# Where operands start modulo 128 bytes: x's transposed parts shifted by 16 bytes, some high parts of the weights by 48

## The chip, the cores and the metric

One core of one Trainium2 chip. The metric is the device time of one execution in microseconds (us), the median of several runs.

## The reference, cut to what matters

A two-layer decoder trunk over 256 positions of width 1024, in float32: latent attention and a PEER expert block, then sparse attention and a second PEER block, each followed by a layer norm.

```
def peer_ffn(x, w_q, subkeys, u, v):              # per 128 positions
    q = (xc @ w_q).reshape(PEER_CHUNK, PEER_HEADS, 2, PEER_DK // 2)
    sc = jnp.einsum("thpd,hpnd->thpn", q, subkeys)  # then top-k: 128 experts a position
    ...
    a = jax.nn.gelu(jnp.einsum("thkd,td->thk", u_e, xc))
    return jnp.einsum("thk,thkd->td", (g * a), v_e)
```

There are 16384 experts. The kernel doesn't gather the rows of u: it multiplies x with the whole table, 128 blocks of 128 experts, and does nearly the same with v.

## The kernel before, in words

**Split products.** Each float32 factor is held as a high part (a float32r copy, made by ScalarE in `_shi`, L119) and a low part (the rest, made by VectorE in `_slo`, L130). A product is high·high + high·low + low·high, three TensorE matmuls on float32r. The weights come as one stream of tiles of 128 x 1024 (`plan`), loaded into `raw`, split into tiles `hi` and `lo` of a ring of four each, and taken by `nxt`.

**x.** The transposed activations lie in the tile `hT` (`new_hT`, L174): for each of eight blocks k of 128 channels, 256 columns of the high part and then 256 of the low part.

**The stages with most matmuls.** In each of the two PEER blocks:

- *Query projection and narrow steps.* `proj_T` (L198) makes 24 matmuls a tile: the weight block is stationary (loaded into the array), 256 columns of `hT` stream past it. This form is used for the queries, for the first steps of u, and for most projections of the sparse attention.
- *Wide steps of u* (`u_step`, from the point where the routing tiles are given up). The high part of the weights meets both parts of x in one matmul of 512 columns: seven of them, then eight matmuls of 256 columns with the low part of the weights, then the eighth of 512.
- *Steps of v* (`v_mm`). Now x-side tiles `W` (128 x 384) are stationary, and 512 columns of `hi` or `lo` stream: ten matmuls a step.

TensorE works in program order, so a matmul of a later stage never starts before those ahead of it.

**Where things start.** A partition's memory is filled pool by pool, in multiples of 32 bytes, so a tile's start follows from the sizes ahead of it. In the built program, modulo 128 bytes: `hT` starts at 96, all `hi`, `lo`, `W`, `cT`, `raw` at 32, `oT` at 32 in the first and 96 in the second attention. Columns are taken in blocks of 128 (512 bytes), so each slice of a tile has the tile's own start modulo 128. *Distance* below means: the start of the stationary block that is loaded for the next matmul, less the start of the operand that streams in the present one, modulo 128 bytes. Before, it is 64 in every product of `hT` with `hi` or `lo`, and 0 in those of `cT` with `hi` or `lo` and of `W` with `hi` or `lo`.

Of the kernel before, what the change touches and what calls it, by code (L numbers as in the profile page):

```python
# [12 lines left out]
F32 = mybir.dt.float32  # L13
F32R = mybir.dt.float32r
# [10 lines left out]
P = 128  # L25
S = 256
D = 1024
KC = D // P
# [6 lines left out]
FIRST, NEXT = 44, 10  # L35
GT = 64
ND = S - GT
RING, LEAD = 6, 7
AHEAD = 12
GB = 0.8  # L40
# [3 lines left out]
class Kern:  # L44
# [5 lines left out]
    def plan(self):  # L50
        I, L = self.I, []
        self.v0s, self.spare, self.pairs = [], None, {}
        if "mla" in self.parts:
            L += [I["a_w_in"][k] for k in range(KC)]
            L += [I["a_wk"][i] for i in range(2)]
            L += [I["a_wq"][i] for i in range(3)]
            L += [I["a_wv"][i] for i in range(2)]
            L += [I["a_wq"][i] for i in range(3, 6)]
            L += [I["a_wo"][i] for i in range(KC)]
        for l in (0, 1):  # L60
            if l == 1 and "nsa" in self.parts:
                L += [I["s_wv"][i] for i in range(4)]
                L += [I["s_wT"][i] for i in range(4)]
                L += [I["b_wg"]]
                L += [I["s_wT"][i] for i in range(4, 8)]
                L += [I["b_wq"][i] for i in range(4)]
                L += [I["b_wq"][i] for i in range(4, 8)]
                L += [I["b_wo"][i] for i in range(KC)] + [I["b_wo"][i] for i in range(KC // 2)]
            if f"peer{l}" in self.parts:
                L += [I["p_wq"][l, i] for i in range(16)]  # L70
                L += [I["p_u"][l, (P - FIRST + j) % P] for j in range(P)]
                self.v0s.append(len(L))
                o = (len(L) - self.v0s[0]) % 4
                self.pairs.update((len(L) + j, I["p_v"][l, j:j + 2].rearrange("j i d -> i j d")) for j in range(o % 2, P - 1, 2))
                L += [I["p_v"][l, j] for j in range(P)]
        self.stream = L
        self.v0 = self.vb = self.v0s[0]
        self.si = 0
        self.sd = 0
        self.sh = 0  # L80
        self.sl = 0
        self.raws, self.his, self.los = {}, {}, {}
        self.share = False
        self.alt = {}
        self.later, self.now = [], 0
# [25 lines left out]
    def _shi(self, upto):  # L111
        while self.sh <= min(upto, len(self.stream) - 1):
            i = self.sh
            self._sdma(i, True)
            if i in self.alt:
                self.his[i], self.los[i] = self.alt.pop(i)()
            else:
                self.his[i] = self.shl.tile([P, self.raws[i].shape[-1]], F32R, tag="hi", name="hi")
            self.nc.scalar.copy(self.his[i], self.raws[i])  # L119
            self.sh += 1  # L120

# [52 lines left out]
    def new_hT(self):  # L174

        self.spare = None
        self.hTT = self.pers.tile([P, KC, 2, S], F32R, tag="hT", name="hT")
        self.hT = [self.hTT[:, :, i, :] for i in range(2)]

    def prep_tail(self):  # L180
# [261 lines left out]
    def peer(self, l):  # L442
        tc, nc, I = self.tc, self.nc, self.I
        self.v0 = self.v0s.pop(0)
        with ExitStack() as es:
            pool = lambda st, name: st.enter_context(tc.tile_pool(name=name, bufs=1, reuse_waits="tile"))


            A = [(pool(es, "slots0").tile([P, FIRST, ND], F32, name="A0"), P - FIRST, FIRST)]

            def slot(j):
                for x, j0, n in A:
                    if j0 <= j < j0 + n:
                        return x[:, j - j0, :]
# [5 lines left out]
            gat = pool(es, "gather")  # L460
            gidx = gat.tile([P, 2, P // 2], U32, name="gidx")
            ggate = gat.tile([P, P // 2], F32, name="ggate")
            gw = gat.tile([P, P // 2], F32, name="gw")
            gel = [gat.tile([P, 4], F32, name=f"gel{m}") for m in range(16)]
            gacc = gat.tile([P, D], F32, name="gacc")
            grow, gtable = {}, I["p_v"].rearrange("l j i d -> (l j i) d")
# [145 lines left out]
            def g_gen(hot):  # L612

                b4 = [P, 2, P, 2]
                for t0 in range(0, ND, 4):
                    while len(gq) == 2:
# [76 lines left out]
            for n in range(4, 17):  # L693
                cur = []
                if n < 16:
                    hi, lo = self.nxt()
# [39 lines left out]
            def u_fin(x):  # L736
# [12 lines left out]
                if n:  # L749
                    nc.scalar.activation(ps[:, 0:n], ps[:, 0:n], AF.Gelu)  # L750
                    due.append((y[:, 0:n], ps[:, 0:n]))
                if n < ND:
                    nc.scalar.activation(y[:, n:ND], ps[:, n:ND], AF.Gelu)  # L753
                if j % 4 == 0:
                    gst.append(gat.tile([P, 4, GT], F32, tag="gst", name="gst", bufs=2))
                nc.scalar.activation(gst[-1][:, j % 4, :], ps[:, ND:S], AF.Gelu)  # L756
                if j % 4 == 3:
# [8 lines left out]
            def w_hi(j):  # L766
                if j < P:
                    WW[j] = late[0].tile([P, 3 * P], F32R, tag="w", name="W", bufs=10) if late else W[0][:, j % 5, :]
                    nc.scalar.copy(WW[j][:, 0:ND], slot(j))  # L769

# [13 lines left out]
            for j in range(P):  # L784
                x = u_step(j)
                u_fin(pu)
                pu = x
                g_flush(2)
                run_side(1.6 if len(A) == 1 else GB)
                if not side and len(A) == 1:  # L790
                    es_r.close()
                    hot = self.pr8.tile([P, 2, 3, 2, P, 2], F16, tag="r8", name="hot")
                    A.append((self.pr8.tile([P, NEXT, ND], F32, tag="r8", name="A2"), 0, NEXT))
                    n = P - FIRST - NEXT
                    A.append((pool(es_1, "slots1").tile([P, n, ND], F32, name="A1"), NEXT, n))
                    side.append(g_gen(hot))
                if done["g"] == ND and j >= P - 3 and not W:
                    w_start()
# [44 lines left out]
            for j in range(P):  # L843
# [9 lines left out]
                hi, lo = self.nxt(j < P - 2)  # L853
# [54 lines left out]
    def mla(self, hN, gb):  # L908
# [3 lines left out]
        with es:  # L912
            pool = lambda *a, **k: es.enter_context(tc.tile_pool(*a, reuse_waits="tile", **k))
            mp = pool(name="mla", bufs=1)
# [2 lines left out]
            keep = pool(name="mkeep", bufs=4)  # L917
            cN = mp.tile([P, 2, 768], F32, name="cN")
            kpN = mp.tile([P, 2, 32], F32, name="kpN")
            cT = [mp.tile([P, 6, S], F32R, tag=f"cT{i}", name=f"cT{i}") for i in range(2)]  # L920
            qT = mp.tile([96, NH, S], F32, name="qT")
            kT = mp.tile([96, NH, S], F32, name="kT")
            vN = mp.tile([P, 2, D], F32, name="vN")
            oT = [mp.tile([P, KC, S], F32R, tag=f"oT{i}", name=f"oT{i}") for i in range(2)]
            gq = mp.tile([P, 6], F32, name="gq")
            rN = mp.tile([P, 2, 64], F32, name="rN")
# [9 lines left out]
            for k in range(KC):  # L936
                hi, lo = self.nxt(k <= KC - 3)
# [66 lines left out]
            for b in range(2):  # L1004
                hi, lo = self.nxt(False)
# [14 lines left out]
            for b in range(2):  # L1020
                hi, lo = self.nxt()
# [21 lines left out]
            for k in range(2):  # L1043
                hi, lo = self.nxt()
# [14 lines left out]
            for st in range(NH + 3):  # L1059
                self.tick()  # L1060
                h = st
                if h < NH:
                    s = self.ps()
                    q, k = qT[:, h, :], kT[:, h, :]
# [6 lines left out]
                if 0 <= h < NH:  # L1071
                    p, m = pr.pop(h)
# [7 lines left out]
                if 0 <= h < NH and h % 2 == 1:  # L1080
                    pvp = self.ps()
                    pp = [pts.pop(h - 1), pts.pop(h)]
                    for w in range(2):
                        for e in range(2):
                            o = pvp[64 * e:64 * e + 64, 0:S]
# [6 lines left out]
                if h < NH:  # L1092
# [4 lines left out]
                    p = prob.tile([P, 384], F32, tag="p", name="p")  # L1097
# [4 lines left out]
                if 0 <= h < NH:  # L1102
                    p, m = pr[h]
# [560 lines left out]
```

## Time and profile before

| | us |
|---|---|
| median of 3 runs | 1760.79 |
| lowest, highest | 1753.84, 1761.01 |
| the profiled execution | 1749.82 |
| its span, first to last instruction | 1748.0 |

The profiled execution has its own time, and its span leaves out 1.8 us around it. The rows below are read from this execution.

### The profile page before, as it was taken

The page shows a single profiled execution, that of the slowest core. Times are in us where ns is not written, and L with a number is a line of the kernel's source. Part 1 is how long each engine was busy: PE and PEld are TensorE (multiplying, and loading weights), DVE is VectorE, ACT ScalarE, POOL GpSimd, SP SyncE. Part 2 cuts the span into 40 slices and gives each one's busy share as a digit, 9 for nine tenths or more (in the row PEclk, how much of TensorE's full clock was granted, in tenths as well). Part 3 has the DMA queues.
Part 4 walks back from the last instruction along what each step waited for, and adds up shares of the span by engine and source line. Part 5 has one row for each costly group of instructions (what it writes and reads, how often), then busy time and mean ns, then how long its engine had stood idle before and what let it go on. Part 6 is the DMA issues. An engine that isn't in the chain of part 4 may idle for free.

```text
span 1748.0 us, 30707 instructions
## 1 busy us (share of the span) xinstructions
PE 1703.1 (97%) x10610; PEld 1478.1 (85%) x10610; DVE 1553.4 (89%) x3675; ACT 1042.9 (60%) x2267; POOL 481.4 (28%) x441
## 2 busy tenths in 40 slices
PE   7999999999999999999997999999999999999997
PEld 6879999888888788888785789998888888888886
DVE  5778988989998899999778789988899998999998
ACT  6646555766666555556466755556666666555554
POOL 2110002000001777761341210001000005777740
PEclk9999999999999999999999999999999999999999
DMA  7535667555556899999572265657555557999993
GB/s 246 169 128 195 193 204 261 186 178 181 187 183 251 309 391 370 367 360 332 179 268 67 95 206 176 205 184 275 176 181 186 184 183 290 401 383 369 361 363 110
DMA packets 118619, 416.66 MB, mean 238 GB/s; under 512 B 16032, under 2 KB 18112, under 8 KB 117376
## 3 DMA queue, kind: packets, MB, share of 16 engines
q1 hardware_dynamic: 88976, 322.60, 54.2%
q0 software_dynamic: 29488, 92.10, 14.1%
q8 instruction: 84, 1.38, 0.3%
q14 instruction: 71, 0.58, 0.1%
HBM read 400.49 MB, written 13.63 MB: 237 GB/s over the span
## 4 chain that ended last, share of the span: by engine, by line
PE 72%; issue 16%; DVE 6%; DMA 2%; ACT 2%; POOL 1%; SPq 0%; POOLq 0%; ACTq 0%; DVEq 0%
PE acc L196 36%; PE mm L196 35%; PE mm L223 1%; DVE lo L130 1%; DMA raw<-p_wq 1%; POOL actD L758 1%; DVE keep L130 1%; DMA xT<-xT 0%; POOL row L472 0%; ACT hi L119 0%; POOL gel L476 0%; DMA gel<-actD,gidx 0%; DVE gacc L486 0%; DVE W L774 0%; DMA actD<-gst 0%
## 5 line engine op out<-in xcount | busy, mean ns | idle before, releaser
L119 ACT CAST hi<-raw 128x1024 fp32r<-128x1024 f32 (+1 forms) x463 | 484.6, 1049 | 244.6 <-PE acc L196 99.8
L196 PE MATMUL mm<-hT,hi 128*128 128x256 f32 (+1 forms) x3360 | 612.8, 328 | 0.0
L130 DVE TENSOR_TENSOR lo<-raw,hi 128x1024 fp32r<-128x1024 f32 (+1 forms) x459 | 558.3, 1220 | 32.6 <-ACT hi L119 30.9
L196 PEld LDWEIGHTS mm<-hT,hi 128*128 128x128 f32 x3360 | 483.2, 188 | 46.3 <-issue 1.2
L196 PE MATMUL acc<-hi,W 128*128 128x512 f32 x1452 | 408.8, 390 | 0.0
L196 PEld LDWEIGHTS acc<-hi,W 128*128 128x128 f32 x1452 | 273.2, 188 | 57.0
L196 PEld LDWEIGHTS mm<-hT,lo 128*128 128x128 f32 x2376 | 306.7, 188 | 15.9
L196 PE MATMUL mm<-hT,lo 128*128 128x256 f32 x2376 | 320.0, 277 | 0.0
L196 PE MATMUL acc<-lo,W 128*128 128x512 f32 x968 | 299.6, 391 | 1.8 <-DVE lo L130 1.8
L758 POOL DMA_DIRECT2D actD<-gst x64 | 34.8, 544 | 783.9 <-ACT gst L756 783.9
L472 POOL DMA_INDIRECT row<-p_v,gidx x128 | 191.7, 1498 | 117.8 <-DVE gacc L486 79.9
L196 PEld LDWEIGHTS acc<-lo,W 128*128 128x128 f32 x968 | 181.7, 188 | 41.4 <-DVE lo L130 4.1
L119 ACT CAST hi<-spare 128x1024 fp32r<-128x1024 f32 x122 | 128.1, 1050 | 113.9 <-PE acc L196 100.8
L476 POOL DMA_INDIRECT gel<-actD,gidx x128 | 165.7, 1294 | 50.0 <-issue 36.6
L486 DVE SCALAR_TENSOR_TENSOR gacc<-row,gw,gacc 128x1024 f32<-128x1024 f32 x126 | 161.4, 1281 | 1.1
L130 DVE TENSOR_TENSOR lo<-spare,hi 128x1024 fp32r<-128x1024 f32 x122 | 148.8, 1220 | 5.4 <-ACT hi L119 4.5
L750 ACT ACTIVATE mm<-mm 128x192 f32<-128x192 f32 (+23 forms) x170 | 41.1, 242 | 122.4 <-DVE mm L748 122.4
L774 DVE TENSOR_TENSOR W<-A,W 128x128 fp32r<-128x128 f32 (+1 forms) x512 | 107.6, 252 | 1.8 <-ACT W L769 1.8
L748 DVE TENSOR_TENSOR mm<-mm,half 128x256 f32<-128x256 f32 x174 | 74.5, 428 | 15.4 <-ACT half L747 15.0
L769 ACT CAST W<-A 128x192 fp32r<-128x192 f32 x256 | 88.0, 345 | 0.0
L647 DVE SCALAR_TENSOR_TENSOR A<-acc,A 128x176 f32<-128x176 f32 (+16 forms) x268 | 56.1, 274 | 28.6 <-PE acc L196 25.6
L753 ACT ACTIVATE A<-mm 128x192 f32<-128x192 f32 (+23 forms) x244 | 67.3, 276 | 7.8 <-DVE mm L748 2.8
(275 smaller groups left out, 1759.1 us busy)
## 6 DMA issues: line engine op xcount, KB each, us to landing
raw<-p_u SPq DMA_DIRECT2D x256, 512.0 KB, 4.0
spare<-p_v SPq DMA_DIRECT2D x64, 1024.0 KB, 8.8
raw<-p_v SPq DMA_DIRECT2D x63, 1024.0 KB, 8.7
raw<-p_wq SPq DMA_DIRECT2D x32, 512.0 KB, 4.1
actD<-gst POOLq DMA_DIRECT2D x64, 128.0 KB, 3.9
raw<-b_wo SPq DMA_DIRECT2D x12, 512.0 KB, 3.8
raw<-a_wo SPq DMA_DIRECT2D x8, 512.0 KB, 4.6
raw<-s_wT SPq DMA_DIRECT2D x8, 512.0 KB, 5.6
```

The lines of the kernel that those rows point to most:

```text
L119: self.nc.scalar.copy(self.his[i], self.raws[i])
L130: e.tensor_tensor(self.los[i], raw, self.his[i].bitcast(F32), op=OP.subtract)
L196: self.nc.tensor.matmul(out, a, b, start=start, stop=stop)
L472: nc.gpsimd.indirect_dma_start(out=t, out_offset=None, in_=gtable, in_offset=bass.IndirectOffsetOnAxis(ap=gidx[:, 0, c:c + 1], axis=0))
L476: nc.gpsimd.indirect_dma_start(out=gel[c // 4][:, c % 4:c % 4 + 1], out_offset=None, in_=gplaces, in_offset=bass.IndirectOffsetOnAxis(ap=g ...
L486: nc.vector.scalar_tensor_tensor(gacc, t, gw[:, c:c + 1], gacc, op0=OP.mult, op1=OP.add)
L647: nc.vector.scalar_tensor_tensor(y, pv[:, j0:j0 + m], 1.0 / GS, y, op0=OP.mult, op1=OP.mult)
L748: nc.vector.tensor_tensor(ps[:, 0:S], ps[:, 0:S], t, op=OP.add)
L753: nc.scalar.activation(y[:, n:ND], ps[:, n:ND], AF.Gelu)
L758: nc.gpsimd.dma_start(self.actD[:, jj - 3:jj + 1, :], gst.pop())
L769: nc.scalar.copy(WW[j][:, 0:ND], slot(j))
L774: nc.vector.tensor_tensor(WW[j][:, o:o + c.stop - c.start], slot(j)[:, c], WW[j][:, c].bitcast(F32), op=OP.subtract)
```

## The change

It adds bytes ahead of some operands and moves no instruction: each engine has the same instructions in the same order with the same waits.

- `hT` gets 32 bytes more, and its data start 16 bytes into the tile.
- Each `hi` tile gets 128 bytes more. Where the tile's number is in the set `near`, the data start 48 bytes into it. `near` holds the stream's tiles of the first projection, of the value projections and output projections (`a_wv`, `s_wv`, `b_wo`), and of the wide steps of u that are prepared after the switch to them.
- The tile `gw` is given up: the gated factor of the gathered rows is written over `ggate`.
- Two pads of 64 bytes in the first attention.

With the growth of the tiles ahead, the starts modulo 128 bytes become: `hT` 112; `hi` 64, or 112 in `near`; `lo`, `raw` and `W` 64; `cT` 0; `oT` 64 and 0. In the built program the distances are then:

| product (streams, columns; loaded next) | before | after | matmuls |
|---|---|---|---|
| `hT` 512; `hi` of `near` | 64 | 0 | 1128 |
| `hT` 512; other `hi`, `lo`, other | 64 | 80 | 262 |
| `hT` 256; `hi`, `lo` | 64 | 80 | about 4150 |
| `hT` 256 with `lo`; `hi` of `near` | 64 | 0 | 168 |
| `cT` 256; `hi`, `lo` | 0 | 64 | 187 |
| `hi`, `lo` 512; `W` | 0 | 0 | 2556 |
| `hi` 512 or 288; `hT` | 64 | 0 or 48 | 151 |
| `lo` 512 or 288; `hT` | 64 | 48 | 77 |
| `hi`, `lo` 512; `cT`, `oT` | 0 or 64 | 0, 16 or 64 | 168 |

A distance of 80 modulo 128 is 48 bytes in the other direction.

```
+NEAR = 12
...
         self.v0s, self.spare, self.pairs = [], None, {}
+        self.near = set()
         if "mla" in self.parts:
+            self.near.update(range(KC))
             L += [I["a_w_in"][k] for k in range(KC)]
...
+            self.near.update(range(len(L), len(L) + 2))
             L += [I["a_wv"][i] for i in range(2)]
...
+                self.near.update(range(len(L), len(L) + 4))
                 L += [I["s_wv"][i] for i in range(4)]
...
+                self.near.update(range(len(L), len(L) + KC + KC // 2))
                 L += [I["b_wo"][i] for i in range(KC)] + [I["b_wo"][i] for i in range(KC // 2)]
...
-                self.his[i] = self.shl.tile([P, self.raws[i].shape[-1]], F32R, tag="hi", name="hi")
+
+                n, o = self.raws[i].shape[-1], NEAR if i in self.near else 0
+                self.his[i] = self.shl.tile([P, n + 32], F32R, tag="hi", name="hi")[:, o:o + n]
...
-        self.hTT = self.pers.tile([P, KC, 2, S], F32R, tag="hT", name="hT")
+        t = self.pers.tile([P, 2 * KC * S + 8], F32R, tag="hT", name="hT")
+        self.hTT = t[:, 4:4 + 2 * KC * S].rearrange("p (k a t) -> p k a t", k=KC, a=2)
...
-            gw = gat.tile([P, P // 2], F32, name="gw")
+            gw = ggate
...
                     es_r.close()
+                    self.near.update(range(self.si, self.v0))
...
+            mp.tile([P, 16], F32, name="pad")
             cT = [mp.tile([P, 6, S], F32R, tag=f"cT{i}", name=f"cT{i}") for i in range(2)]
...
+            mp.tile([P, 16], F32, name="pad2")
             oT = [mp.tile([P, KC, S], F32R, tag=f"oT{i}", name=f"oT{i}") for i in range(2)]
```

## Rows read from the trace of the kernel before

**Rows 1.** The page: busy time by engine, and TensorE's granted clock in tenths.

```profile
PE 1703.1 (97%) x10610; PEld 1478.1 (85%) x10610; DVE 1553.4 (89%) x3675; ACT 1042.9 (60%) x2267; POOL 481.4 (28%) x441
...
PEclk9999999999999999999999999999999999999999
```

**Rows 2.** The page's chain that ended last; the chain's longest piece in narrow steps.

```profile
PE 72%; issue 16%; DVE 6%; DMA 2%; ACT 2%; POOL 1%; SPq 0%; POOLq 0%; ACTq 0%; DVEq 0%
...
171.92 87.77 PE mm L196 x772
```

**Rows 3.** Busy us by window: narrow steps, wide steps, v of each layer.

```profile
core 0: us, PE busy (x) PEld busy (x) DVE busy (x) ACT busy (x) POOL busy (x), PEclk, DMA share, GB/s
172.00:262.00 90.00, 90.00 (x794) 90.00 (x795) 84.63 (x347) 49.40 (x101) 3.79 (x7) 1.00 0.64 198
300.00:400.00 100.00, 100.00 (x682) 87.28 (x681) 88.44 (x230) 66.89 (x188) 4.32 (x8) 1.00 0.59 193
580.00:700.00 120.00, 120.00 (x530) 99.35 (x530) 118.56 (x203) 68.55 (x105) 90.34 (x67) 1.00 1.00 383
1460.00:1680.00 220.00, 220.00 (x972) 182.25 (x971) 213.16 (x364) 125.83 (x194) 160.07 (x117) 1.00 0.98 368
```

**Rows 4.** Timeline of PE in a wide step: start us, us, what, how many.

```profile
401.68 2.02 PE L196 MATMUL mm<-hT,hi 128*128 128x512 f32 x8
403.54 1.07 PE L196 MATMUL mm<-hT,lo 128*128 128x256 f32 x8
404.45 2.02 PE L196 MATMUL mm<-hT,hi 128*128 128x512 f32 x8
```

**Rows 5.** Timeline of PE in the first attention's up-projections (`cT`), at two places.

```profile
39.38 1.12 PE L196 MATMUL mm<-cT,hi 128*128 128x256 f32 x8
...
46.58 1.12 PE L196 MATMUL mm<-cT,hi 128*128 128x256 f32 x8
```

**Rows 6.** Timeline of PE where fm is loaded and w streams (whole float32).

```profile
891.77 1.94 PE L196 MATMUL acc<-w,fm 128*60 128x256 f32 x16
...
892.25 1.46 PE L196 MATMUL acc<-w,fm 128*60 128x256 f32 x12
```

**Rows 7.** Groups of PE by shape: count, then busy us, mean ns.

```profile
L196 PE MATMUL mm<-hT,hi 128*128 128x512 f32 x1392 | 364.1, 397 | 0.0
L196 PE MATMUL mm<-hT,lo 128*128 128x256 f32 x2376 | 320.0, 277 | 0.0
...
L196 PE MATMUL mm<-hT,hi 128*128 128x256 f32 x1968 | 248.6, 279 | 0.0
...
L196 PE MATMUL mm<-cT,hi 128*128 128x256 f32 x128 | 19.5, 287 | 2.2 <-ACT cT L979 1.2 <-ACT kpT L1000 0.9
...
L196 PE MATMUL mm<-cT,lo 128*128 128x256 f32 x64 | 10.9, 283 | 0.0
```

**Rows 8.** The page's groups of the two splitting operations.

```profile
L119 ACT CAST hi<-raw 128x1024 fp32r<-128x1024 f32 (+1 forms) x463 | 484.6, 1049 | 244.6 <-PE acc L196 99.8
...
L130 DVE TENSOR_TENSOR lo<-raw,hi 128x1024 fp32r<-128x1024 f32 (+1 forms) x459 | 558.3, 1220 | 32.6 <-ACT hi L119 30.9
```

More of the change, by code (lines that the diff above doesn't have):

```diff
@@ L37 @@
 ND = S - GT
+NEAR = 12
 RING, LEAD = 6, 7
@@ L52, in plan @@
         self.v0s, self.spare, self.pairs = [], None, {}
+        self.near = set()
         if "mla" in self.parts:
+            self.near.update(range(KC))
             L += [I["a_w_in"][k] for k in range(KC)]
@@ L56, in plan @@
             L += [I["a_wq"][i] for i in range(3)]
+            self.near.update(range(len(L), len(L) + 2))
             L += [I["a_wv"][i] for i in range(2)]
@@ L61, in plan @@
             if l == 1 and "nsa" in self.parts:
+                self.near.update(range(len(L), len(L) + 4))
                 L += [I["s_wv"][i] for i in range(4)]
@@ L67, in plan @@
                 L += [I["b_wq"][i] for i in range(4, 8)]
+                self.near.update(range(len(L), len(L) + KC + KC // 2))
                 L += [I["b_wo"][i] for i in range(KC)] + [I["b_wo"][i] for i in range(KC // 2)]
@@ L117, in _shi @@
             else:
-                self.his[i] = self.shl.tile([P, self.raws[i].shape[-1]], F32R, tag="hi", name="hi")
+                n, o = self.raws[i].shape[-1], NEAR if i in self.near else 0
+                self.his[i] = self.shl.tile([P, n + 32], F32R, tag="hi", name="hi")[:, o:o + n]
             self.nc.scalar.copy(self.his[i], self.raws[i])
@@ L176, in new_hT @@
         self.spare = None
-        self.hTT = self.pers.tile([P, KC, 2, S], F32R, tag="hT", name="hT")
+        t = self.pers.tile([P, 2 * KC * S + 8], F32R, tag="hT", name="hT")
+        self.hTT = t[:, 4:4 + 2 * KC * S].rearrange("p (k a t) -> p k a t", k=KC, a=2)
         self.hT = [self.hTT[:, :, i, :] for i in range(2)]
@@ L462, in peer @@
             ggate = gat.tile([P, P // 2], F32, name="ggate")
-            gw = gat.tile([P, P // 2], F32, name="gw")
+            gw = ggate
             gel = [gat.tile([P, 4], F32, name=f"gel{m}") for m in range(16)]
@@ L791, in peer @@
                     es_r.close()
+                    self.near.update(range(self.si, self.v0))
                     hot = self.pr8.tile([P, 2, 3, 2, P, 2], F16, tag="r8", name="hot")
@@ L919, in mla @@
             kpN = mp.tile([P, 2, 32], F32, name="kpN")
+            mp.tile([P, 16], F32, name="pad")
             cT = [mp.tile([P, 6, S], F32R, tag=f"cT{i}", name=f"cT{i}") for i in range(2)]
@@ L923, in mla @@
             vN = mp.tile([P, 2, D], F32, name="vN")
+            mp.tile([P, 16], F32, name="pad2")
             oT = [mp.tile([P, KC, S], F32R, tag=f"oT{i}", name=f"oT{i}") for i in range(2)]
```

## The prediction

> **What bounds the kernel now.** I read the page first. TensorE is busy 97% of the span, VectorE 89%, and the granted clock is at the upper of its two levels (2.4 GHz) in all forty slices [rows 1], so the clock has next to nothing to give. The chain that ended last is 72% TensorE [rows 2]. An engine's share is an average, so next comes busy time by stage. In narrow steps, wide steps and v TensorE is busy for the whole window [rows 3]: it never waits, and a matmul that takes less time moves all that follows, until another engine becomes the bound. The next one is VectorE: 94% in narrow steps (84.63 of 90.00), 88% in wide steps, 99% in v (118.56 of 120.00) [rows 3]. In v the DMA engines are full too (share 1.00).
>
> So the question is the pace of a matmul: window over count, or the distance of two starts in the timeline. A row's "mean ns" is no pace, since matmuls overlap: 256 columns have a mean of 277 to 279 ns [rows 7], and 794 of them fit into 90.00 us [rows 3]. The paces, with the distance modulo 128 as the kernel's description gives it:
>
> - 256 columns at 64: 90.00 / 794 = 113.4 ns [rows 3]; in a wide step (404.45 - 403.54) / 8 = 113.8 ns [rows 4].
> - 256 columns at 0: between the two rows of `cT` stand sixty matmuls (five rounds of eight and four), and 7.20 us / 60 = 120.0 ns [rows 5].
> - 512 columns at 64: (403.54 - 401.68) / 8 = 232.5 ns [rows 4].
> - 512 columns at 0: 120.00 / 530 = 226.4 ns, and 220.00 / 972 = 226.3 ns [rows 3].
>
> The same shape has two paces at two distances, and the order is opposite: 64 is the better one for 256 columns, 0 for 512. While one block streams, the next is being loaded: weight loads are busy 90.00 of 90.00 us in narrow steps [rows 3]. So a clash of the two reads is a plausible reason, and their distance a plausible cause. But the rows differ in more than the distance (other tiles, other operands), so it is read from them, not proved.
>
> The Trainium skill speaks against it: by "TensorE: Matmul & The Clock Gate", section "Part 2: What happens when you issue a matmul", TensorE has two independent read ports, and the load of the next weights steals nothing from the running matmul. By that rule a start modulo 128 can't matter and the change would give 0 us. The trace's 120.0 against 113.4 ns for one shape speaks against the rule, without excluding another reason.
>
> **The change, part by part.** No instruction is added, taken away or moved, so each part is a count of matmuls times a change of pace. Counts are from the built program and agree with the groups [rows 7]: 1392 / 8 = 174 wide steps.
>
> 1. *512 columns, `hT` past high parts, 64 to 0: 1128 matmuls.* 232.5 to 226.4 ns: -6.1 x 1128 = -6.9 us. Bounds: 0 (distance is not the reason) and -6.9; no row shows a faster matmul of 512. I take -6.9.
> 2. *256 columns, `hT`, 64 to 80: about 4150 matmuls (1968 + 2376 less those of the next item).* No row shows float32r at 80. The worst row for this shape is 120.0 (at 0): +6.6 x 4150 = +27.4 us. The best comes from whole float32, where `fm` is loaded while `w` streams: blocks of `fm` start 240 bytes apart, so the distance runs 0, 112, 96, 80, four records to a block. The first four take 892.25 - 891.77 = 0.48 us, 120 ns each; the other twelve take 1.46 us less the overhang of the last, which is 1.07 - 0.91 = 0.16 us in rows 4, so 1.30 / 12 = 108 ns [rows 4, 6]. So three distances that are no multiple of 64 run clean there, 80 among them. By that row it is -5.4 x 4150 = -22.4 us. Same operands at 64, or other type at 80: the second has the distance in question, and its penalty at 0 is of the same kind, but whole float32 is taken in two records a matmul, another form. I take 110 ns, most of the way to 108: -3.4 x 4150 = -14.1 us.
> 3. *The last low part of a wide step, ahead of a shifted high part, 64 to 0: 168 matmuls.* 113.4 to 120.0: +6.6 x 168 = +1.1 us.
> 4. *`cT`, 0 to 64: 192 matmuls* [rows 7]. 120.0 to 113.4: -1.3 us.
> 5. *262 of 512 columns that go from 64 to 80, and some 400 of the small products with `hT`, `cT`, `oT` in other places.* Some go to 0, some leave it; the rows give 6 ns either way, at most 660 x 6.1 = 4.0 us. I take 0.
> 6. *Writing and reading the shifted tiles.* ScalarE's copy (1049 ns) now writes 48 bytes further, VectorE's subtraction (1220 ns) reads there [rows 8]. ScalarE is busy 55% in narrow steps, and the shifted tiles of u are used in wide steps, where VectorE has 12% left [rows 3]. Even 10% more on 1220 ns, 0.12 us a wide step, stays in that room; without it, it would be 174 x 0.12 = 21 us. I take 0. `gw` written over `ggate` is the same instruction with the same waits: 0.
>
> Does it all arrive? A narrow step is 24 x 113.4 = 2.72 us, VectorE works 84.63 / (794 / 24) = 2.56 us of it. At 110 ns it is 2.64 us: VectorE rises to 97%, still under. At 108 ns (2.59 us) it would be 99%, and some of the last 2 ns would turn into waits. A wide step is shorter by 8 x 6.1 + 8 x 3.4 = 76 ns of about 2.8: VectorE goes to about 91%. The v steps have distance 0 on both sides, so their 226.4 ns stay, which is well, since VectorE and DMA are full there: a faster u stage ends earlier and gives v nothing to run into.
>
> Sum: -6.9 - 14.1 + 1.1 - 1.3 = -21.2 us of the profiled execution's own 1749.8 us (its span of 1748.0 and 1.8 around it): 1728.6, a ratio of 0.988. The profiled execution lies 0.6% under the median of the three runs, 1760.8; by the ratio the median becomes 1739.5.
>
> **The rivals.**
>
> - *512 columns gain, 256 columns don't* (80 is like 64): -6.9 + 1.1 - 1.3 = -7.1 us, 0.4%, median 1753.7. For it: within float32r both multiples of 64 cost something, and nothing shows that a distance between them is clean. Against it: 108 ns at 80 in `fm` [rows 6].
> - *80 is as bad for float32r as 0, so slower.* Part 2 then costs +27.4 us, the sum +20.3, median 1781. For it: the best distance of 512 columns is the worst of 256, so paces don't carry over between forms; `fm` is another form. The place is every narrow step: 24 x 120.0 = 2.88 us instead of 2.72. It decides from 113.4 + 7.1 / 4150 ns = 115.1 ns on; it is beyond 0.5% from 117.2 ns.
> - *The distance is not the cause* (the skill's rule, or a cause in the operands): 0 us, median 1760.8. For it: the rows compare different tiles. Against it: 512 columns of `W` and of `hT` differ by 6.1 ns steadily over both layers, and `fm` changes pace within one tile with nothing but its start changed [rows 6].
> - *VectorE becomes the bound* in narrow steps because its subtraction slows down with the new places. At 10%, 0.12 us a step, it would be 2.68 us against 2.64 and take back 82 steps x 0.04 = 3 us. It changes the size alone.
>
> **How the numbers follow.** About 0.5%, 9 us, is what a measurement of this kernel can tell from no change. Chances: both gain, 0.68; only 512 columns gain, 0.12; no effect, 0.06; slower by the 256 columns, 0.14. In the first case part 2 lies between -5 and -22.4 us and part 5 within 4 us: a median of 1724 to 1753. With the second case and no effect the range goes to 1761 and leaves out the slower case, 0.14, and a little at the edges. Faster by over 0.5%: the first case but for its weak end, and a bit of the second: 0.70. Within: 0.16. Slower: 0.14.
>
> **What would show it.** A window of narrow steps has 90 us / 110 ns = 818 matmuls in place of 794. In a wide step eight high products take 8 x 226.4 = 1.81 us in place of 1.86, eight low ones 0.88 in place of 0.91. `cT` does sixty in 6.80 us in place of 7.20. The v windows still show 226.4 ns. VectorE's subtraction is still 1220 ns, and TensorE is still busy all through. The prediction is wrong if the narrow pace at 80 is 113 ns or more, or if it falls and VectorE is at 100% there.

## The result and the profile after

The changed kernel takes 1776.4 us (median of six executions) against 1759.24 us for the kernel before on the same chip: a ratio of 1.0097, 95% interval [1.0078, 1.0115]. One of the six took 2425.48 us at a granted clock of 0.65 and is left out of the ratio; the other five lie between 1773.8 and 1777.1 us. The kernel is slower by 17 us. The forecast was 1739 with a range to 1761; the sign is that of the rival in which 80 bytes is as bad for float32r as 0 (1781 us).

The page of the kernel after: busy time by engine, the chain that ended last by engine, and the groups of the two splitting operations.

```profile
PE 1734.9 (98%) x10610; PEld 1500.9 (85%) x10610; DVE 1556.8 (88%) x3675; ACT 1044.2 (59%) x2267; POOL 481.9 (27%) x441
...
PE 92%; DVE 3%; ACT 2%; DMA 2%; issue 1%; SPq 0%; ACTq 0%
...
L127 ACT CAST hi<-raw 128x1024 fp32r<-128x1024 f32 (+1 forms) x463 | 483.6, 1047 | 258.6 <-PE acc L205 102.3
...
L138 DVE TENSOR_TENSOR lo<-raw,hi 128x1024 fp32r<-128x1024 f32 (+1 forms) x459 | 558.1, 1219 | 46.9 <-ACT hi L127 42.8
```

The same 10610 matmuls take 32 us more of TensorE. VectorE and ScalarE are as they were: 1219 and 1047 ns for a split where [rows 8] have 1220 and 1049. TensorE's share of the chain is 92%, where [rows 2] had 72%; but a second profile of the kernel before (next section) has 89%, so this difference is not put down to the change.

The chain of the kernel after in the narrow steps of layer 0:

```profile
174.59 92.02 PE mm L205 x772
```

The piece of [rows 2] has the same 772 matmuls in 87.77 us. 92.02 / 772 = 119.2 ns a matmul, where it was 113.7.

Windows of the kernel after: narrow steps, wide steps, v of layer 1 (which begins some 20 us later than in [rows 3], so the window is moved).

```profile
172.00:262.00 90.00, 89.98 (x757) 89.79 (x757) 85.62 (x351) 48.90 (x99) 3.79 (x7) 1.00 0.62 196
300.00:400.00 100.00, 100.00 (x675) 87.51 (x674) 86.79 (x220) 66.60 (x188) 4.37 (x8) 1.00 0.62 206
...
1480.00:1700.00 220.00, 220.00 (x955) 179.04 (x954) 210.23 (x358) 124.59 (x194) 163.58 (x117) 1.00 0.97 362
```

Fewer matmuls fit into each window: 757 in place of 794, 675 of 682, and in v 955 of 972, 230.4 ns each where [rows 3] gave 226.3. The last is a surprise: the prediction had v stay at 226.4 ns. TensorE is busy all through and the granted clock is 1.00, so it is the pace and no wait.

The timeline of PE in a wide step of the kernel after, and in the up-projections with `cT`:

```profile
400.92 2.02 PE L205 MATMUL mm<-hT,hi 128*128 128x512 f32 x8
402.78 1.12 PE L205 MATMUL mm<-hT,lo 128*128 128x256 f32 x8
403.74 2.01 PE L205 MATMUL mm<-hT,hi 128*128 128x512 f32 x8
```

```profile
40.67 1.07 PE L205 MATMUL mm<-cT,hi 128*128 128x256 f32 x8
...
47.47 1.07 PE L205 MATMUL mm<-cT,hi 128*128 128x256 f32 x8
```

Eight high products take 1.86 us, as in [rows 4], though their distance went from 64 to "0". Eight low ones take 0.96 us in place of 0.91: 120 ns. Only `cT` did what was forecast: sixty matmuls in 6.80 us, 113.3 ns, where [rows 5] gave 120.0.

### The profile page after: what moved, and what is told of

It is laid out like the page before. It is cut to its first block, busy times and chain, and to the rows that moved or that the text cites. A ratio compares the mean times of both kernels' runs of the same rounds, so it can differ in the third digit from the quotient of the medians.

```text
span 1775.2 us, 30707 instructions
## 1 busy us (share of the span) xinstructions
PE 1734.9 (98%) x10610; PEld 1500.9 (85%) x10610; DVE 1556.8 (88%) x3675; ACT 1044.2 (59%) x2267; POOL 481.9 (27%) x441
## 4 chain that ended last, share of the span: by engine, by line
PE 92%; DVE 3%; ACT 2%; DMA 2%; issue 1%; SPq 0%; ACTq 0%
PE mm L205 51%; PE acc L205 40%; PE mm L232 1%; DMA raw<-p_wq 1%; ACT hi L127 1%; DVE lo L138 0%; DMA xT<-xT 0%; DMA raw<-s_wT 0%; DMA spare<-p_v 0%; DVE hN L300 0%; DVE bnst L278 0%; DVE hN L282 0%; ACT p L1557 0%; DVE qs L1373 0%; DVE m L1550 0%
## 5 line engine op out<-in xcount | busy, mean ns | idle before, releaser
L127 ACT CAST hi<-raw 128x1024 fp32r<-128x1024 f32 (+1 forms) x463 | 483.6, 1047 | 258.6 <-PE acc L205 102.3
L205 PE MATMUL mm<-hT,hi 128*128 128x256 f32 (+1 forms) x3360 | 620.2, 330 | 0.4 <-ACT hi L127 0.4
L138 DVE TENSOR_TENSOR lo<-raw,hi 128x1024 fp32r<-128x1024 f32 (+1 forms) x459 | 558.1, 1219 | 46.9 <-ACT hi L127 42.8
L205 PEld LDWEIGHTS mm<-hT,hi 128*128 128x128 f32 x3360 | 491.6, 188 | 46.6 <-issue 1.2
L205 PE MATMUL mm<-hT,lo 128*128 128x256 f32 x2376 | 332.0, 282 | 0.0
L205 PEld LDWEIGHTS mm<-hT,lo 128*128 128x128 f32 x2376 | 316.1, 189 | 15.0
L205 PE MATMUL acc<-lo,W 128*128 128x512 f32 x968 | 303.5, 394 | 0.1
L127 ACT CAST hi<-spare 128x1024 fp32r<-128x1024 f32 x122 | 128.3, 1051 | 113.7 <-PE acc L205 92.4
L495 DVE SCALAR_TENSOR_TENSOR gacc<-row,ggate,gacc 128x1024 f32<-128x1024 f32 x126 | 161.2, 1279 | 1.1
L138 DVE TENSOR_TENSOR lo<-spare,hi 128x1024 fp32r<-128x1024 f32 x122 | 148.8, 1219 | 8.5 <-ACT hi L127 8.2
```

Source lines behind the costliest of these rows:

```text
L138: e.tensor_tensor(self.los[i], raw, self.his[i].bitcast(F32), op=OP.subtract)
L205: self.nc.tensor.matmul(out, a, b, start=start, stop=stop)
L495: nc.vector.scalar_tensor_tensor(gacc, t, gw[:, c:c + 1], gacc, op0=OP.mult, op1=OP.add)
```

## The experiments

In what follows a pace is the mean time from one matmul's start to the next one's start, over all matmuls of that shape and place that waited for nothing.

### A second look at both kernels

No edit. How much of the difference belongs to the kernel, and how much to the execution?

> The kernel before, profiled a second time. If a pace belongs to the kernel's addresses: 113.4 to 114.5 ns for 256 columns of hT, 232.8 for 512, 226.8 in v, as in its first profile. If paces differ from run to run with the same addresses, these move by ns, and the 2.7 to 3.4 ns by which move128 differed from the first profile mean nothing.

> The changed kernel, profiled a second time. If a pace belongs to the addresses: 119 ns for 256 columns, 232.3 for 512, 230.6 in v again, within half a ns.

One execution each: 1755.56 and 1775.41 us. The kernel after repeats the paces of its large groups to 0.1 ns. The kernel before doesn't. Its narrow steps of layer 1, from 1100 to 1160 us, in the profile that the prediction was made from, and then in the second one:

```profile
1100.00:1160.00 60.00, 60.00 (x531) 60.00 (x530) 55.33 (x198) 33.28 (x67) 2.70 (x5) 1.00 0.63 196
```

```profile
1100.00:1160.00 60.00, 60.00 (x512) 60.00 (x511) 54.01 (x192) 32.05 (x66) 2.70 (x5) 1.00 0.64 203
```

60.00 / 531 = 113.0 ns and 60.00 / 512 = 117.2 ns: at a distance of 64 this shape has two paces, and it keeps one of them over a whole stage. The execution behind the prediction had the good one in both layers, the second in layer 0 alone. So the second one (nearer to the median) is what the kernel after is compared with. Time by stage, in us, from the first matmul of each stage to the first of the next (v: to its last):

| | to wide steps, layer 0 | wide | v | to wide steps, layer 1 | wide | v |
|---|---|---|---|---|---|---|
| before, first profile | 285.5 | 265.1 | 295.6 | 335.2 | 265.1 | 291.0 |
| before, second | 285.3 | 265.1 | 294.7 | 342.1 | 265.1 | 290.9 |
| after | 292.7 | 268.5 | 296.2 | 343.3 | 268.5 | 295.5 |
| `stride` (below) | 284.5 | 264.0 | 296.2 | 335.9 | 264.4 | 295.4 |
| `after_s` (below) | 290.5 | 268.5 | 291.9 | 341.6 | 268.5 | 291.0 |
| `odd144` (below) | 285.2 | 264.7 | 297.7 | 335.2 | 265.6 | 291.2 |

After less before (second): +7.4, +3.4, +1.5, +1.2, +3.4, +4.6 us. All stages lose. The first number is the least sure: the second profile of the kernel after has 290.9 us there, which makes it +5.6.

### TensorE alone, eight starts by eight

A kernel that computes nothing of the reference: one engine, the same kind of matmul, each operand at eight places 16 bytes apart.

```
for cols in (256, 512):
    for m in range(8):
        for s in range(8):
            acc = ps.tile([P, 512], F32, tag="acc", name="acc")
            for k in range(N):
                c = k % (2048 // cols) * cols
                nc.tensor.matmul(acc[:, 0:cols], st[s][:, k % 8 * P:k % 8 * P + P], mv[m][:, c:c + cols],
```

> TensorE alone: float32r matmuls of 256 and of 512 columns, 24 for each of the 64 pairs of starts of the streaming and of the loaded operand (0, 16 to 112 bytes past a multiple of 128); it computes nothing of the reference. If the distance alone decides, all eight pairs of one distance have one pace: 256 columns 120 ns at 0, 113.4 ns at 64, 119 ns at 80; 512 columns 227 ns at 0, 232 ns at 64. If places decide, the pace changes along a line of equal distance. If neither, all pairs have one pace and the cause lies with the other engines.

The pace does depend on the places: pairs lay between 113 and 120 ns for 256 columns and between 226 and 235 ns for 512, with no other engine at work. But pairs of equal distance modulo 128 didn't agree. So the cause is real and the variable is wrong. Most pairs with the same distance modulo 256 and the same streaming start modulo 32 were equal: 34 of the 40 sets that have more than one pair agree within 0.6 ns (one of the other six holds the slow first products of the run). Not all were. At a distance of 112 from an odd multiple of 16 bytes, one start has 113.3 ns and the three others 118.7. At 64, odd starts have 113.3 and multiples of 32 have 117.8. First 64 from a multiple of 32, then 112 from 16 and from 48 modulo 256:

```profile
34.52 2.99 PE L44 MATMUL acc<-ma,we 128*128 128x256 f32 x24
37.35 2.97 PE L44 MATMUL acc<-ma,wf 128*128 128x256 f32 x24
...
45.84 2.88 PE L44 MATMUL acc<-mb,wa 128*128 128x256 f32 x24
48.56 3.00 PE L44 MATMUL acc<-mb,wb 128*128 128x256 f32 x24
...
96.65 3.01 PE L44 MATMUL acc<-md,wc 128*128 128x256 f32 x24
99.50 3.00 PE L44 MATMUL acc<-md,wd 128*128 128x256 f32 x24
```

From one group's start to the next: 2.83, 2.72 and 2.85 us for 24 matmuls, 117.9, 113.3 and 118.8 ns.

### Moving the places within the kernel

Three edits of the kernel before change nothing but `hT`'s tile: 128 bytes more (`move128`), 32 bytes more (`move32`), or 128 bytes more with the data 16 bytes into it (`ht16`).

```
-        self.hTT = self.pers.tile([P, KC, 2, S], F32R, tag="hT", name="hT")
+        t = self.pers.tile([P, 2 * KC * S + 32], F32R, tag="hT", name="hT")     # move32: + 8
+        self.hTT = t[:, 0:2 * KC * S].rearrange("p (k a t) -> p k a t", k=KC, a=2)  # ht16: 4:4 + ...
```

> The kernel before with everything behind hT 128 bytes later: no start modulo 128 changes. Distance theory and place theory: same time (within 0.3%), narrow steps 113.4 ns, v steps 226.4 ns. If the slower paces of the changed kernel come from another chip or from larger moduli, this one is off 113.4 and 226.4 as well.

> The kernel before with everything behind hT 32 bytes later, hT itself unmoved: hi, lo and W start at 64 as in the changed kernel; distances of W and cT stay 0, that of hT becomes 96. Distance theory: v steps stay at 226.4 ns. Place theory: v steps go to the 230.6 ns of the changed kernel, +4 ns x 2556 = +10 us there alone.

> The kernel before with hT's data 16 bytes later (112) and all else at its old start modulo 128: distance of hT to hi and lo is 48. Both theories: v steps stay at 226.4 ns. Distance theory with a symmetric clash: 256 columns at 48 as slow as at 80, 119 ns, +5.5 ns x 4300 = +24 us. If only 80 is bad, 113 ns or less, within 5 us of before.

Measured: 1.0003 [0.9982, 1.0023], 1.0071 [1.0048, 1.0094] and 1.0066 [1.0042, 1.009]. With nothing but places moved, and other ones than the change's, most of its loss is there: 256 columns at 117.8 and 119.5 ns. `move128` leaves every distance modulo 128 as it was, and still the paces move: 114.5 to 117.2 ns for 256 columns, 232.8 to 229.5 for 512. The two cancel in part in the ratio, so the ratio alone would have hidden it. For 256 columns this shows nothing by itself, since the second profile of the kernel before has the pace of `move128` in its layer 1 (512 matmuls from 1100 to 1160 us in both); the 232.8 ns stand in both profiles.

### The period: one operand in 128 places

Again TensorE alone, nothing of the reference. The streaming operand starts at a multiple of 128 bytes (`map2`) or 112 bytes past one (`map3`); the loaded one moves on by 16 bytes for each accumulator, 2048 bytes in all.

```
for cols, rounds in ((256, 3), (512, 2)):
    for d in range(ND):
        name = "d" + chr(97 + d // 16) + chr(97 + d % 16)
...
        nc.tensor.matmul(acc[:, 0:cols], w[:, q * P + 4 * d:q * P + 4 * d + P], m[:, OFF + q * 512:OFF + q * 512 + cols],
```

> TensorE alone, with the steps that u has (2048 bytes on the streaming side, 512 on the loaded side), one streaming start, and a loaded start that moves in 128 steps of 16 bytes over 2048 bytes; it computes nothing of the reference. A period of 128 bytes: the paces repeat every 8 steps, 120 ns at 0 and 113.3 at 64 for 256 columns. A period of 512: every 32 steps, 113.3 at 64 and 576, about 117 at 192.

> The table of TensorE alone again, with the streaming operand 112 bytes past a multiple of 128 (where the changed kernel has hT) and the same distances; it computes nothing of the reference. If the distance modulo 256 is all, every row is that of the first table: 256 columns 113.3 at 64, 118.9 at 80; 512 columns 226.7 at 0. If the start itself counts as well, the rows differ, most where a start is no multiple of 32 bytes.

The timeline of `map2`. The accumulator's last letter is the distance in steps of 16 bytes (a is 0, e is 64, f is 80, i is 128, m is 192), the letter before it the turn of 256 bytes.

```profile
56.19 3.04 PE L40 MATMUL dba<-m,w 128*128 128x256 f32 x24
59.06 3.01 PE L40 MATMUL dbb<-m,w 128*128 128x256 f32 x24
...
67.57 2.89 PE L40 MATMUL dbe<-m,w 128*128 128x256 f32 x24
70.29 3.01 PE L40 MATMUL dbf<-m,w 128*128 128x256 f32 x24
73.15 2.98 PE L40 MATMUL dbg<-m,w 128*128 128x256 f32 x24
...
112.95 2.89 PE L40 MATMUL dce<-m,w 128*128 128x256 f32 x24
115.67 3.01 PE L40 MATMUL dcf<-m,w 128*128 128x256 f32 x24
...
433.14 3.79 PE L40 MATMUL dba<-m,w 128*128 128x512 f32 x16
436.77 3.80 PE L40 MATMUL dbb<-m,w 128*128 128x512 f32 x16
...
462.76 3.90 PE L40 MATMUL dbi<-m,w 128*128 128x512 f32 x16
466.49 3.90 PE L40 MATMUL dbj<-m,w 128*128 128x512 f32 x16
```

256 columns: 2.87 us for 24 at a distance of 0 (119.6 ns), 2.72 at 64 (113.3), 2.86 at 80 (119.2). 512 columns: 3.63 us for 16 at 0 (226.9), 3.73 at 128 (233.1). The pattern comes back after 256 bytes and not after 128: dbe and dce both take 2.72 us, and so for each of the 16 places in all eight turns, to 0.02 us, but for the first group of 256 and the first of 512 columns. From the other start, `map3`:

```profile
70.23 3.02 PE L40 MATMUL dbf<-m,w 128*128 128x256 f32 x24
73.09 2.99 PE L40 MATMUL dbg<-m,w 128*128 128x256 f32 x24
75.92 2.89 PE L40 MATMUL dbh<-m,w 128*128 128x256 f32 x24
78.64 3.04 PE L40 MATMUL dbi<-m,w 128*128 128x256 f32 x24
81.52 2.88 PE L40 MATMUL dbj<-m,w 128*128 128x256 f32 x24
84.24 3.03 PE L40 MATMUL dbk<-m,w 128*128 128x256 f32 x24
...
431.69 3.88 PE L40 MATMUL dba<-m,w 128*128 128x512 f32 x16
435.41 3.79 PE L40 MATMUL dbb<-m,w 128*128 128x512 f32 x16
```

80 takes 2.86 us here too, 119.2 ns. 112 and 144 take 2.72 (113.3 ns). And 512 columns at 0 take 3.72 us, 232.5 ns: from this start 0 is no good place for them. The start of `hT` in the kernel after is 112.

### High tiles 4224 bytes apart, alone

The kernel before, with only the growth of each `hi` tile by 128 bytes (and `gw` on `ggate`, for room). No start changes modulo 128.

```
+                n = self.raws[i].shape[-1]
+                self.his[i] = self.shl.tile([P, n + 32], F32R, tag="hi", name="hi")[:, 0:n]
```

> The kernel before with hi tiles of 4224 bytes in place of 4096, no start modulo 128 changed (gw is written over ggate to make room). Distance modulo 128 decides: 0 us, v steps 226.8 ns. A period longer than 128 bytes decides: the hi tiles now stand at 0, 128, 256 and 384 modulo 512 from W and from the other operands, and v steps go towards the changed kernel's 230.6 ns, up to +10 us in all, 256 columns towards move128's 117 ns.

Ratio 0.9998 [0.998, 1.0016]. But v has the new pace, and all of it. The windows of v in layer 1, first of `stride`, then of `after_s` (the changed kernel with `hi` tiles 4352 bytes apart, further below):

```profile
1460.00:1680.00 220.00, 220.00 (x955) 179.05 (x955) 209.88 (x356) 123.51 (x191) 162.32 (x115) 1.00 0.98 362
```

```profile
1480.00:1700.00 220.00, 220.00 (x973) 182.21 (x972) 214.82 (x366) 126.42 (x195) 159.24 (x114) 1.00 0.98 369
```

955 is 230.4 ns, 973 is 226.1. With 4352 bytes (a multiple of 256) the loss is gone. So the loss in v comes from the tiles' step. How the step does it is not shown. Of four buffers 4224 bytes apart every second one is at 128 modulo 256 from `W`, where `map2` has 233.1 ns in place of 226.9, and the mean of the two, 230.0, looks like an explanation. The trace doesn't bear it out: in `stride` the high products at 0 take 229.8 ns, those at 128 take 230.4, and the low products, whose distance is 0 as before, take 231.6 in place of 226.8. One of these low pairs:

```profile
1501.10 0.63 PE L197 MATMUL acc<-lo,W 128*128 128x512 f32 x2
1501.57 1.08 PE L197 MATMUL acc<-hi,W 128*128 128x512 f32 x4
```

0.47 us for two is 235 ns each. In a step whose tiles all lie at 0, the first seven products still take between 224 and 236 ns (means over the 57 such steps of layer 1), and only the last three take 226.7. The step ahead of it has its high tile at 128. So what ran before counts, and not the present pair of places alone.

The narrow steps of `stride` say the same:

```profile
1100.00:1160.00 60.00, 60.00 (x530) 60.00 (x529) 55.33 (x198) 33.31 (x67) 2.70 (x5) 1.00 0.62 196
```

Every second tile is at 192 there, where `map2` has 117.8 ns (`dbm`), and still its products run at 113.7 ns like the others at 64.

In `stride` v of layer 1 is 4.4 us longer than before; in the profiled execution the good pace of its narrow steps (335.9 us ahead of the second wide stage) makes up for it. That execution is the fastest of ten (1752.7 us, median 1757.0), so for the ratio of 1 it is not shown.

### Good places by the table, first attempts

`cand`: the kernel before with the four high parts in one tile, 4096 bytes apart, and those of the wide steps 64 bytes ahead, at a distance of 0 modulo 256. `after256`: the kernel after with one tile in the same way and everything behind `hT` moved by 128 bytes. In both, the first tile behind a switch lies over the edge of its neighbour: 16 columns of a weight tile (12 in `after256`) hold other values, so their products aren't the reference's.

```
-                self.his[i] = self.shl.tile([P, self.raws[i].shape[-1]], F32R, tag="hi", name="hi")
+                n, o = self.raws[i].shape[-1], 48 + self.hslot % 4 * D + (0 if i in self.near else 16)
+                self.hslot += 1
+                self.his[i] = self.hring[:, o:o + n]
```

> Made by the 256-byte table: the kernel before, the four hi places in one tile of 4096-byte steps, the high parts of the wide steps 64 bytes earlier, so that 512 columns of hT have distance 0 modulo 256, 256 columns keep 64 and v keeps 0. Period of 256 bytes: 512 columns fall from 232.8 to 226.7 ns in the 1128 products, 256 columns stay at 113.3 to 115.5, the 168 products ahead of a shifted tile go to 120; -6.9 + 1.1 = -6 us, ratio 0.996 to 0.998. Distance modulo 128 alone: the same. If 512 columns keep 232.8 here too, the table of TensorE alone doesn't carry over to the kernel.

> The changed kernel with its distances made true modulo 256: hi in 4096-byte steps, everything behind hT 128 bytes later, so that the shifted high parts stand at 0 from hT, the others at 208 (48 bytes the other way) and W at 0. Period of 256 bytes: v back to 226.7 ns, 256 columns at the table's 116.7 to 117.3 in place of 119.1, 512 columns between 226.7 and 230: about 15 us under the changed kernel, within 0.4% of before. Distance modulo 128 alone: nothing changes against the changed kernel, since modulo 128 every distance is the same.

Ratios 1.016 [1.0131, 1.0189] and 1.0283 [1.025, 1.0315]: both slower than the kernel that they were made from. As tests of time they say little, since one tile brought waits. TensorE's waits in `cand` (engine and line, what it waited for: us, times, longest):

```profile
PE acc L199 <- ACT hi L122: 21.0, 5, 6.6
PE mm L199 <- ACT hi L122: 8.5, 6, 2.6
```

In the second profile of the kernel before the first is 6.3 us, once, and the other isn't there. Their paces count all the same: 512 columns at 0 in `cand` 230.4 ns, not 226.9; in `after256`, where each of these products has a distance of exactly 0 from the start of 112, 232.7 ns, as `map3` has it.

### Separate tiles 4352 bytes apart

`cand3` does what `cand` meant, with tiles of their own. `after_s` is the kernel after with the same step of tiles; nothing else of the change is undone. Room comes from one buffer less of `half` and a small tile put into another.

```
-                self.his[i] = self.shl.tile([P, self.raws[i].shape[-1]], F32R, tag="hi", name="hi")
+                n, o = self.raws[i].shape[-1], 48 if i in self.near else 0     # after_s: NEAR
+                self.his[i] = self.shl.tile([P, n + 64], F32R, tag="hi", name="hi")[:, o:o + n]
...
-                    t = gat.tile([P, S], F32, tag="half", name="half", bufs=2)
+                    t = gat.tile([P, S], F32, tag="half", name="half", bufs=1)
```

> As cand, but with four hi tiles of their own, 4352 bytes apart (a multiple of 256), the high parts of the wide steps 192 bytes into them, and one buffer for half in place of two to make room. Period of 256 bytes and starts that are multiples of 32: 512 columns 226.7 to 227 ns in the wide steps (232.8 before), 256 columns between 113.3 and 117.8 as in before, v 226.8; wide stages 265.1 - 87 x 6 x 6 ns = 262 us each, in all 5 to 7 us less than before. If the 230.4 ns of cand were the distance itself and not the waits on its one tile, 512 columns stay at 230.4 here, and the gain is 2 us.

> The changed kernel with hi tiles 4352 bytes apart in place of 4224 (one buffer for half, one small constant moved, to make room): W and hi are again at 0 modulo 256, all else keeps its place modulo 128. Period of 256 bytes: v 226.8 ns in place of 230.6, worth 4 to 5 us in the second layer and 1.5 in the first, where v doesn't wait for TensorE alone; 256 columns stay at 119 ns (80), 512 columns at 232 to 233 (128 from a start of 112). So about 5 us under the changed kernel and 11 to 13 us over before. Distance modulo 128: the same time as the changed kernel, 230.6 ns in v.

`after_s`: 1.0066 [1.0043, 1.009], 1765.44 us. Undoing the step alone gives back 11 of the 17 us by medians, about 5 by the two ratios (1.0097 and 1.0066, each against the kernel before on its own chip); by stage it is 4.3 and 4.5 us in the two v stages, 2.2 us in the first stage (where two profiles of the kernel after differ by 1.8) and 1.7 us ahead of layer 1's wide steps. What is left is the pace of 256 columns at 80, still 119.1 ns.

`cand3`: 0.9999 [0.9986, 1.0013]. 512 columns at 0 modulo 256 take 230.4 ns, 2.1 less than the same products before (232.5) and not the 6 of the table. The eight products of 256 columns between them, at 64 as before, take 116 to 118 ns in place of 113 to 114, and the wide stages take 268.4 us (2.9 of it one wait) and 265.7, where 262 was expected. Its profiled narrow steps had the poorer pace in both layers. No gain.

### Good places from an odd start

The last two take the start of the change (an odd multiple of 16 bytes) and the places that `map3` calls good: 256 columns at 112 (`odd112`) or 144 (`odd144`), the wide steps' 512 at 192, high tiles 4352 bytes apart.

```
+        t = self.pers.tile([P, 2 * KC * S + 24], F32R, tag="hT", name="hT")    # odd112: + 16
+        self.hTT = t[:, 4:4 + 2 * KC * S].rearrange("p (k a t) -> p k a t", k=KC, a=2)
...
+                n, o = self.raws[i].shape[-1], 12 if i in self.near else 0     # odd112: 20
+                self.his[i] = self.shl.tile([P, n + 64], F32R, tag="hi", name="hi")[:, o:o + n]
```

> x's parts start at an odd multiple of 16 bytes as after the change (48 modulo 128), but the distance is 112 modulo 256 for every product of 256 columns and 192 for the wide steps' 512 columns (high tiles 4352 bytes apart, 80 bytes later for those steps). My theory (the table of TensorE alone for an odd start: 113.3 ns at 112, 226.7 ns for 512 columns at 192): narrow steps 113 to 118 ns, not 119; 512 columns 226.7 to 230.4 ns against 232.8; W keeps 226.8; ratio 0.994 to 1.001. If an odd start as such were the loss, or the paces of the table didn't carry over: 119 ns in the narrow steps and a ratio of 1.006 to 1.01.

> The same with a distance of 144 modulo 256 (16 modulo 128) for every product of 256 columns, 192 for the wide steps' 512 columns. My theory (table, odd start: 113.3 ns at 144, 120.0 at 128, 119.4 at 80): as the run with 112, ratio 0.994 to 1.001, narrow steps 113 to 118 ns. A period of 128 bytes with 64 as the only good place would give 119 to 120 ns and a ratio of 1.006 to 1.01.

`odd112`: 1.0035 [1.0022, 1.0049]. `odd144`: 0.9969 [0.9954, 0.9983], 1750.41 us against 1755.23: the one version of this study that beats the kernel before. Their narrow steps of layer 1, `odd112` first:

```profile
1100.00:1160.00 60.00, 60.00 (x508) 60.00 (x507) 56.71 (x207) 32.23 (x67) 2.71 (x5) 1.00 0.65 199
```

```profile
1100.00:1160.00 60.00, 60.00 (x532) 60.00 (x531) 55.46 (x197) 32.34 (x67) 2.71 (x5) 1.00 0.64 203
```

118.1 and 112.8 ns. 16 modulo 128 (which is 144 modulo 256) is as good as 64; so 64 isn't the one good place, and an odd start isn't itself the loss. But 113.3 ns doesn't hold for 112. In the built `odd112` `hT` starts at 48 modulo 256, and for that start and distance `map` had 118.7 ns with TensorE alone. A profiled `odd144` has a stage of 335.2 us ahead of the second wide steps, where the kernel before has 335.2 or 342.1; its wide steps gain nothing (264.7 and 265.6 against 265.1), though 512 columns fell to 228.2 ns. So its 5 us look like the good pace of the narrow steps kept. Whether it is always kept at 144 isn't shown by one profile.

What the table (TensorE alone, `map2` and `map3`, behind the first eight products of each group) says and what the kernels had, in ns:

| kernel | `hT`'s start mod 32 | 256 columns at (mod 256) | alone | in the kernel | 512 columns at | alone | in the kernel |
|---|---|---|---|---|---|---|---|
| before | 0 | 64 | 113.3 | 114.5, 115.2 | 64 | 233.0 | 232.8 |
| `move128` | 0 | 192 | 117.7 | 117.2 | 192 | 229.0 | 229.5 |
| `stride` | 0 | 192 | 117.7 | 114.1 | 192 | 229.0 | 228.9 |
| `move32` | 0 | 96 | 117.3 | 117.8 | 96 | 234.3 | 233.7 |
| `ht16` | 16 | 176 | 119.9 | 119.5 | 176 | 231.6 | 231.2 |
| after | 16 | 80 | 119.4 | 119.3 | 0 | 233.4 | 231.7 |
| after | 16 | 208 | 118.4 | 118.4 | 128 | 232.7 | 232.9 |
| `cand3` | 0 | 64 | 113.3 | 116.4 | 0 | 226.7 | 230.4 |
| `odd112` | 16 | 112 | 113.3 | 118.6 | 192 | 226.7 | 228.7 |
| `odd144` | 16 | 144 | 113.3 | 115.1 | 192 | 226.7 | 228.2 |

The poor places agree within 0.6 ns in all rows but two (1.7, and 3.6 in `stride`). The good ones are good in the kernel only in part. It goes the other way too: the 214 products of 512 columns at 144 in `odd144` take 226.3 ns, and 231.3 with TensorE alone. This is not the work of the other engines alone: `map` has 117.8 ns at 64 and 118.7 at 112, and for 512 columns at 0 from an odd start 229.9 where `map3` has 233.4, with TensorE alone and other steps between the blocks. One place can have two paces, so the table is a list of what was met, not a rule.

## Why the prediction was wrong

**Part 2, the step that failed.** "I take 110 ns, most of the way to 108": the pace of whole float32 at 80 was carried over to float32r. For float32r 80 bytes is one of the poor places, 119.1 ns in the kernel (the mean of 80 and 208 modulo 256) and 119.2 with TensorE alone, so in place of -14.1 us it is (119.1 - 114.5) x 4150 = +19 us against the first profile, +16 against the second (115.2). The text had named the reason against it itself ("another form"), and the bound of +27.4 held it. The pace from which that rival is beyond 0.5%, 117.2 ns, was passed.

The 108 ns themselves were misread. In [rows 6] stands a first group of 16 records. Its first four take 0.48 us, and this was put down to a distance of 0. The next group of the same tile loads blocks that start at 32, 16, 0 and 112, at distances of 64, 48, 32 and 16:

```profile
896.67 1.94 PE L196 MATMUL acc<-w,fm 128*60 128x256 f32 x16
...
897.15 1.47 PE L196 MATMUL acc<-w,fm 128*60 128x256 f32 x12
```

Again 0.48 us for the first four records. By the starts in the trace, the first matmul of either group takes 0.264 us and every later one 0.216 (two records each), whatever the distance. So `fm` gave no sign that 80 is good, and none that the pace follows the distance, though the prediction used it for both.

**Part 1.** -6.9 us was forecast, and 232.3 ns in place of 232.5 for these products is -0.2 us. That places set the pace held; that the distance modulo 128 does it didn't. The `hi` tiles that grew by 128 bytes lie at 0 and at 128 modulo 256 in turn, and from the changed start 0 is poor for 512 columns (`map3` 232.5, `after256` 232.7). And where 0 modulo 256 was had from the old start (`cand3`), the mixed wide step gave 230.4, not 226.4: so placed it would be -2.4 us, and the 256 columns beside them lost.

**"The v steps have distance 0 on both sides, so their 226.4 ns stay": wrong.** It is 0 modulo 128, and for half of the high tiles 128 modulo 256; with the new step of the tiles all products of `hi` and `lo`, moved or not, take 230.7 ns on the mean in place of 226.8, +3.86 x 2420 = 9.3 us of work, of which 1.5 and 4.6 us arrive; in layer 0's v other things limit the kernel before as well (294.7 us against 290.9 in layer 1).

**Parts 3 and 4.** The 168 matmuls took 120.1 ns (+0.9 us); `cT` went from 119.8 to 114.8 ns, -1.0 us. Both as forecast. In `map2` too, 64 is good for 256 columns and 0 is not, and 0 is good for 512 from this start and 64 is not. For `cT` there is luck in it: in the built kernel two thirds of its products lie at 192 modulo 256, where TensorE alone has 117.7 ns and `after_s` 117.8.

**Parts 5 and 6.** The splits cost what they did. VectorE isn't the bound in the narrow steps (85.62 of 90.00 us). Of the 262 products of 512 columns, 214 went from 234.6 to 230.7 ns and the 48 whose next matmul is another kind's from 230.0 to 237.0: -0.5 us together.

**The sum**, with measured paces against the second profile: +16.2 - 0.2 + 0.9 - 1.0 + 9.3 - 0.5 = +24.7 us of work. The spans differ by 1775.2 - 1753.8 = 21.4. The difference of 3.3 fits what of v's 9.3 us doesn't arrive (9.3 - 1.5 - 4.6 = 3.2). With the second profile of the kernel after the spans differ by 19.8, so the close fit is partly luck.

**The rule against the change.** By the Trainium skill ("TensorE: Matmul & The Clock Gate", "Part 2: What happens when you issue a matmul") the load of the next weights takes nothing from the running matmul; by that the starts wouldn't matter. The forecast set it aside, and there it was right: in `map2` one shape takes 113.3 or 120.0 ns with nothing but the loaded block's start changed. No run here shows what slows them.

**What stays open.** What decides between two paces at one place (113 or 118 ns at 64, for a whole stage and in one execution but not the next; 113.3 or 118.7 at 112); how the products that ran before come into it; why the start modulo 32 counts; by what path the tiles' step slows v.

## What to carry to other kernels

A pace read at two places gives two points, not a law: before building on "modulo 128", sweep one operand's start through a few hundred bytes with the engine alone, in the form that the kernel uses; one run gives the poor places and their prices. A good place in such a table is a candidate only: here two attempts at good places brought nothing or a loss, and one brought 0.3%. Before a pace is put down to a place, look whether other rows of the same form at other places have it too, as those of `fm` did. A tile's growth moves every buffer of its ring, so the step between buffers belongs to the list of what a change of places touches. And where a kernel has two paces by chance, two profiles of it are needed before a difference of a few us is put down to anything.

## What was not expected of the hardware

- With TensorE alone and one streaming start (`map2`), the pace of float32r matmuls repeats in the loaded block's place with a period of 256 bytes: 16 places in eight turns, equal to 0.02 us a group but for the first; 113.3 to 120.0 ns for 256 columns, 226.7 to 234.3 ns for 512.
- The start of the streaming operand counts too: 512 columns at a distance of 0 take 226.9 ns from a multiple of 128 bytes and 232.5 ns from 112 past it.
- At a distance of 64 the same program runs a whole stage at 113.0 or at 117.2 ns a matmul, differently from one execution to the next, about 7 us in the stage ahead of layer 1's wide steps (335.2 and 342.1 us). TensorE alone has two paces at one place as well: at 112 from a start of 112, 113.3 ns in `map3` and 118.7 in `map`, which has other steps between its blocks.
- A pace outlasts the places that made it: with every second high tile of v at 128 modulo 256, the steps at 0 run seven products at 224 to 236 ns before they come down to 226.7, and low products that haven't moved take 231.6 in place of 226.8 (`stride`).
